# Latent keys and values of a gated-mixer layer, made with positions on partitions instead of channels on partitions, with another order of the first loads and steps and another price for narrow transfers in the planner

## The chip, the core and the metric

The program runs on one core of one Trainium2 chip. A time is the device time of one execution in microseconds. The kernel before took 1004.93 us in the median of 3 runs (999.37 to 1005.2). The profile is that of one further execution, which took 1003.57 us; the span between its first and last instruction is 1001.8 us, so 1.77 us lie around the span.

The engines are named as in the profile: PE (TensorE, with PEld for its weight loads), DVE (VectorE), ACT (ScalarE), POOL (GpSimd) and SP (SyncE, which issues nearly all DMAs).

## The reference, cut to what matters

One layer with 1024 positions plus 16 learned "meta" positions in front (L = 1040), width 1024, all in float32:

```python
h = rms_norm(h_res, pre_norm_g)            # over the 1024 channels of a position
z = h @ w_in                               # one projection, 7328 columns
(pv, pg, cq, ckv, kr, mg, cu, cg, sbcx, sg, gl) = split_cols(z)
...
kv = rms_norm(ckv, kv_norm_g) @ w_ukv      # ckv: 128 columns, over which the norm goes
k_rope = apply_rope(kr, cos, sin)          # kr: 32 columns
k = concat([k_nope, broadcast(k_rope)])    # 8 heads of 64 + 32
...
m = sum_i sigmoid(g_i) * y_i ;  out = h_res + rms_norm(m @ w_o, post_norm_g)
```

Four mixers (pooling, latent attention, a depthwise convolution of 31 taps, a short convolution) read slices of `z`. The change concerns the 160 columns `ckv` (128) and `kr` (32): the latent that keys and values are made from, and the one rotary key that all heads share.

## The kernel before, in words

**Three stages.** Stage one (until about 653 us) normalises x, projects it by `w_in`, and runs the mixers' element-wise work beside the projection. Stage two (about 653 to 870 us) is the attention of 8 heads in two halves of 512 queries each, with the output projections of three branches ("fills") between its matmuls. Stage three is the output projection of the attention, the gated sum, `w_o` and the last norm.

**The projection.** The normalised x is turned so that channels are on partitions, and split into a rounded high part and a rest (`hi`, `lo`), so that a float32 product is three matmuls (hi by hi, hi by lo, lo by hi). x is taken as a matrix of two by two blocks (512 channels by 512 positions: `B11`, `B21`, `B12`, `B22`), and 256 columns of `w_in` make a two by two block of weights; a Winograd scheme does the block product with 7 products instead of 8 from the blocks and their sums `T1` to `T4` (`unit`, `sums_of`, `prep`). `B12` and `T3` share a buffer, which holds `B12` first. A product is 12 matmuls: 4 groups of 128 channels by 3. The weights stand still in PE, up to 512 positions move. The first pairs of columns go in two pieces of 256 and 272 positions (`U0`, `U1`).

**The first 160 columns.** They are done first and directly, since `T1` to `T4` aren't made yet (`plain`): for each of 2 pieces and 2 halves of the positions, 24 matmuls for the 128 latent columns (`ps_pa<-B,kv`) and 24 for the rotary key (`ps_pb<-B,kr`, 64 columns, because its two halves are put beside it in swapped order). The result has channels on partitions and goes to `z_ckv` and `z_kr` in DRAM. Much later `task_kv` reads them back, multiplies `kr` by the cosines and sines, and normalises the latent; since the norm goes over partitions, `rs_row` sums the squares with matmuls by a column of ones and turns the result back with transposes.

**The start.** x comes in 8 tiles of 128 positions (`load_x`, 512 KB each) on SP's queue, with the weights of the 160 columns between. `parts(t)` squares two tiles on ACT, takes the root on POOL (one `pow` for both tiles), scales on DVE, transposes on PE (`ps_x`, `ps_y`), and splits: hi on ACT, lo on DVE. POOL makes the block sums (`x<-x`) in place.

**What orders the work.** No order is written out. `Plan` records every operation with a cost in ns, and at each `flush` gives each engine, in a simulated time, the ready operation of lowest priority number; `plan.ahead(n)` moves operations up by n places in priority. Each engine then runs its list strictly in that order. Two rules of it bear on the change. First, up to the end of the first pair of columns (`keep_busy`), whenever the plan has nothing for PE it puts in a transpose of the identity that nobody reads (`ps_w<-ident`); these are instructions like any other and run even if the real work is ready by then. Second, a DMA has a planned length (L279), bytes times a rate over 16 engines, one after the other, and work that needs it is planned after that. The side work of stage one (`task_kv`, `task_q`, `task_conv` and others) are generators that are pumped a step at a time between products.

In the attention, `load_kv` brings the keys of the next head (`kt<-k`, 64 partitions, 520 KB) once the head before last has been read for the last time, since there are two buffers (`kt0`, `kt1`); `maxima` reads the keys first (`ps_s<-kt,qt`), `attend` next (`ps_s<-qt,kt`). The names in the profile are these program names without numbers; all recorded operations have the line L332.

Of the kernel before, what the change touches and what calls it, by code (L numbers as in the profile page):

```python
# [21 lines left out]
F32 = mybir.dt.float32  # L22
# [171 lines left out]
class Plan:  # L194
# [243 lines left out]
def trunk_kernel(ctx, tc, a):  # L438
# [47 lines left out]
    POOL.memset(f(ends), 0.0)  # L486

    z_dram = {}
    for n in ("a0", "a1", "g0", "g1", "ckv", "kr", "pv0", "pv1", "c0", "c1", "x0", "x1"):
# [67 lines left out]
    def prep(c):  # L557
# [10 lines left out]
        w = {n: blk(src, n) for n, src in (("A11", a11), ("S2", s2), ("S1", s1), ("S3", a21))}  # L568
        sub(DVE, s2, a12, s2)
        w.update({n: blk(src, n) for n, src in (("A12", a12), ("A22", a22), ("S4", s2))})  # L570
        return w

    def product(ps, w, b, c0, n, start, stop):

        for k in range(KH):
            s = slice(c0, c0 + n)
            xh, xl = HB[b][:, 0, k, s], HB[b][:, 1, k, s]
            last = stop and k == KH - 1
            PE.matmul(ps, w[:, 0, k], xh, start=start and k == 0, stop=False, skip_group_check=True)
            PE.matmul(ps, w[:, 0, k], xl, start=False, stop=False, skip_group_check=True)  # L580
            PE.matmul(ps, w[:, 1, k], xh, start=False, stop=last, skip_group_check=True)
# [127 lines left out]
    def load_x(t):  # L709

        xt[t] = (t4([P, D], name="x") if t in (4, 5, 6, 7) else
                 wp.tile([P, D], F32, tag="raw", bufs=3, name="x") if t == 0 else
                 wp.tile([P, D], F32, tag="blk", bufs=7, name="x"))
        SP.dma_start(xt[t], a["x"][0, P * t:P * (t + 1), :])
    g8 = wr.tile([KD, P], F32, tag="wraw", bufs=2, name="g8")

    with plan.slow(-400):
        load_x(0)
        ACT.dma_start(g8, a["pre_norm_g"][0].rearrange("(k p) -> k p", p=P))
        load_x(4)  # L720
        load_x(1)
        load_x(5)
        raw_kv = [wload(i, C_CKV, P + 32) for i in range(2)]
        for t in (2, 6, 3, 7):
            load_x(t)
        xm = wp.tile([NM, D], F32, tag="blk", bufs=7, name="xm")
        SP.dma_start(xm, a["meta_tokens"])
# [34 lines left out]
    def parts(t):  # L762


        for e in range(2):
            square(xt[t + 4 * e], 2 * t + e)
        rsqrt_mean(rsx[:, 2 * t:2 * t + 2], ssx[:, 2 * t:2 * t + 2], D)
        for e, bs in enumerate(((B11, B21), (B12, B22))):
            scaled(xt[t + 4 * e], 2 * t + e)
            for i, b in enumerate(bs):  # L770
                operand_of(b, t, xt[t + 4 * e][:, 512 * i:512 * (i + 1)])
# [9 lines left out]
            operand_of(b, t, src)  # L781

    def meta():
        square(xm, 8)
        rsqrt_mean(rsx[:NM, 8:9], ssx[:NM, 8:9], D)
# [12 lines left out]
        DVE.scalar_tensor_tensor(HB[T1][:, 1, :, 512:], b1, -1.0, f(hi), op0=ALU.mult, op1=ALU.subtract)  # L798
# [18 lines left out]
    parts(0)

    for t in raw_kv:
        POOL.tensor_copy(t[:, :, P + 32:P + 48], t[:, :, P + 16:P + 32])  # L820
        POOL.tensor_copy(t[:, :, P + 48:P + 64], t[:, :, P:P + 16])
    w_kv = [[blk(t[:, :, :P], "kv")] for t in raw_kv]
    kr = wp.tile([P, 2, 2, KH, 64], F32R, tag="blk", bufs=7, name="kr")
# [4 lines left out]
    out_kv = [out_raw(("ckv", "kr"), *u) for u in (U0, U1)]  # L828
    parts(2)
    parts(3)  # L830
# [9 lines left out]
    plain(w_kv, *U1, out_kv[1])  # L840
    for t in range(2, 4):
        operand_of(T3, t, xt[t + 4][:, :512])
    prow = w1([P, P], name="prow")
# [9 lines left out]

    done = {"ckv", "kr"}

    def rs_row(sqs, of, scale=None, tag="x"):

# [235 lines left out]

    def task_kv():

        k0, k1, cs = t4([32, L], name="kr0"), t4([32, L], name="kr1"), t4([32, L], name="kcs")
        for k_, r0, i in ((k0, 0, 0), (k1, 32, 1)):
            ld(k_, z_dram["kr"][r0:r0 + 32, :])  # L1100
            ld(cs, a["trig"][i][:32, :])
            mul(POOL, k_, k_, cs)
            cs = t4([32, L], name="kcs2") if i == 0 else None
        add(POOL, k0, k0, k1)
        yield
        kh, kl = t4([33, L], F32R, name="krh"), t4([33, L], F32R, name="krl")
# [6 lines left out]
            for r, s, n in ((0, 16, 16), (16, 0, 16), (32, 32, 1)):  # L1113
                ld(kr_dram[1][r:r + n, i], t[s:s + n])
        yield
        ckv, sq = t4([P, L], name="ckv"), t4([P, L], name="sqk")
        ld(ckv, z_dram["ckv"])
        ACT.activation(sq, ckv, AF.Square)
        yield
        for n0, n in CH_KV:  # L1120
            rs = yield from rs_row([sq[:, n0:n0 + n]], P)
            DVE.scalar_tensor_tensor(ckv[:, n0:n0 + n], ckv[:, n0:n0 + n], par[:, R_KVG:R_KVG + 1], rs,
                                     op0=ALU.mult, op1=ALU.mult)
        yield
# [68 lines left out]
    def lane(*tasks):  # L1193

        for needs, task, *args in tasks:
# [3 lines left out]
            while True:  # L1199
# [549 lines left out]
```

## Time and profile before

| | |
|---|---|
| median of 3 runs | 1004.93 us (999.37 to 1005.2) |
| profiled execution | 1003.57 us, of it 1001.8 us span |
| PE | 980.2 us busy (98%), 5128 matmuls, 109 of them identity fill |
| PEld | 825.9 us (82%) |
| DVE, ACT, POOL | 657.2 (66%), 463.0 (46%), 701.2 (70%) |
| DMA | 204.54 MB, mean 204 GB/s |
| mean granted PE clock | 0.996 |

How to read it: "busy" counts an engine's own instructions; the profile shows for each what ended the idle time before it. A line of the timeline is "start, length, engine, line, operation, out<-in, form, count", where neighbours of one kind are merged. Matmuls overlap, so the time that one takes from the next is the distance of the starts, not the length shown. "PEclk" is the clock that PE was granted, as a share of the full one.

### The profile page before, as it was taken

Reading aid. Unit: us, or ns where it says so; the run is one execution under the profiler, and the core shown is the slowest. Engines: PE = TensorE matmul, PEld = TensorE weight load, DVE = VectorE, ACT = ScalarE, POOL = GpSimd, SP = SyncE. Lnnn points to the kernel's source line nnn. Section 1 sums busy time; section 2 is a strip of 40 time slices with the busy share of each in tenths; the row PEclk is TensorE's granted clock in tenths of the full one; section 3 lists DMA queues with packets and bytes.
Section 4 is the critical chain, followed back from the end, with each engine's and each line's share of the span. In section 5 each row is a group of like instructions: output and inputs, shape, how many; then the busy total and the mean of one; then the engine's idle time right before and its main releaser. Section 6 shows DMA issues by size and latency. Waiting matters only on the chain. (4 is left out here: it accounts for less than half of the span.)

```text
span 1001.8 us, 15300 instructions
## 1 busy us (share of the span) xinstructions
PE 980.2 (98%) x5128; PEld 825.9 (82%) x5128; DVE 657.2 (66%) x1078; ACT 463.0 (46%) x934; POOL 701.2 (70%) x648
## 2 busy tenths in 40 slices
PE   9999999999999999999999999999989999999996
PEld 9999898889888788777788888878878888788885
DVE  5846686997789769756555223175656656787747
ACT  7543334444444454444445443257656566224631
POOL 6759877766788787698868544236678898536946
PEclk9999999999999999999999999999999999999998
DMA  7269866788778858765665445677678765681624
GB/s 249 85 196 299 269 185 188 234 265 300 238 242 271 259 173 246 229 184 177 197 177 179 132 140 164 227 237 226 181 180 262 209 177 159 227 283 47 219 87 168
DMA packets 128098, 204.54 MB, mean 204 GB/s; under 512 B 19712, under 2 KB 80887, under 8 KB 126674
## 3 DMA queue, kind: packets, MB, share of 16 engines
q1 hardware_dynamic: 123396, 186.79, 60.0%
q10 hardware_dynamic: 4336, 15.73, 4.3%
q8 instruction: 40, 0.66, 0.3%
q0 software_dynamic: 288, 1.05, 0.3%
q14 instruction: 38, 0.31, 0.1%
HBM read 128.98 MB, written 74.56 MB: 203 GB/s over the span
## 5 line engine op out<-in xcount | busy, mean ns | idle before, releaser
L332 PE MATMUL ps_pa<-B,A 128*128 128x512 f32 (+2 forms) x792 | 172.4, 362 | 0.0
L332 PE MATMUL ps_pb<-T,S 128*128 128x512 f32 (+2 forms) x792 | 171.7, 362 | 0.0
L332 POOL TENSOR_TENSOR A<-raw,A 128x512 fp32r<-128x512 f32 x84 | 114.9, 1371 | 72.3 <-ACT A L332 59.4
L332 POOL TENSOR_TENSOR S<-ss,S 128x512 fp32r<-128x512 f32 x84 | 117.0, 1401 | 60.4 <-ACT S L332 58.9
L332 PEld LDWEIGHTS ps_pa<-B,A 128*128 128x128 f32 x792 | 134.4, 188 | 23.5
L332 PEld LDWEIGHTS ps_pb<-T,S 128*128 128x128 f32 x792 | 134.0, 188 | 23.9 <-issue 0.5
L332 POOL TENSOR_TENSOR pt<-p,pt 128x512 fp32r<-128x512 f32 (+1 forms) x96 | 96.6, 1031 | 37.2 <-PE ps_s L332 20.7
L332 ACT ACTIVATE S<-ss 128x512 fp32r<-128x512 f32 x84 | 51.9, 629 | 104.2 <-DVE ss L332 54.1
L332 PE MATMUL ps_y<-bo,whl 128*128 128x512 f32 x288 | 90.6, 411 | 0.3
L332 DVE SCALAR_TENSOR_TENSOR ps_w<-conv,par,ps_w 128x512 f32<-128x512 f32 x116 | 87.2, 752 | 2.3
L332 PE MATMUL ps_pc<-B,S 128*128 128x512 f32 (+2 forms) x396 | 87.5, 364 | 0.5 <-DVE z L332 0.5
L332 PE MATMUL ps_pd<-T,A 128*128 128x512 f32 (+2 forms) x396 | 87.0, 364 | 0.0
L332 PE MATMUL ps_pc<-T,S 128*128 128x512 f32 (+2 forms) x396 | 84.7, 361 | 0.0
L332 PEld LDWEIGHTS ps_pd<-T,A 128*128 128x128 f32 x396 | 67.0, 188 | 12.8 <-issue 1.4
L332 PEld LDWEIGHTS ps_pc<-B,S 128*128 128x128 f32 x396 | 66.9, 188 | 12.8 <-DVE z L332 0.7
L332 PEld LDWEIGHTS ps_pc<-T,S 128*128 128x128 f32 x396 | 67.1, 188 | 11.8
L332 PE MATMUL ps_s<-qt,kt 97*128 97x512 f32 (+4 forms) x336 | 70.1, 326 | 1.0 <-ACT qt L332 0.7
L332 ACT ACTIVATE A<-raw 128x512 fp32r<-128x512 f32 x84 | 52.7, 627 | 37.0 <-PE ps_pd L332 30.1
L332 PE MATMUL ps_o<-pt,vt 128*128 128x512 f32 (+7 forms) x288 | 69.7, 344 | 0.1
L332 ACT ACTIVATE p<-ps_s 128x512 f32<-128x512 f32 (+4 forms) x112 | 49.6, 443 | 35.2 <-DVE ps_s L332 14.6
L332 PEld LDWEIGHTS ps_s<-qt,kt 97*128 97x128 f32 (+1 forms) x336 | 54.1, 176 | 12.0 <-ACT qt L332 1.8
L332 DVE TENSOR_REDUCE mxs<-ps_s 128x1 f32<-128x144 f32 (+6 forms) x112 | 56.1, 507 | 7.7 <-PE ps_s L332 5.4
(354 smaller groups left out, 1905.2 us busy)
## 6 DMA issues: line engine op xcount, KB each, us to landing
raw<-in_w_in_dram SPq DMA_DIRECT2D x56, 512.0 KB
th<-th SPq DMA_DIRECT2D x32, 512.0 KB
th<-z ACTq DMA_DIRECT2D x30, 512.0 KB
v<-vhl SPq DMA_DIRECT2D x16, 384.0 KB
qt<-q SPq DMA_DIRECT2D x16, 384.0 KB
vt<-v SPq DMA_DIRECT2D x8, 768.0 KB
bo<-bo SPq DMA_DIRECT2D x6, 1024.0 KB
kt<-k SPq DMA_DIRECT2D x8, 520.0 KB
```

Of the source, the lines that this page charges most:

```text
L332: getattr(self.handle[o["eng"]], o["op"])(*map(real, o["args"]), **{k: real(v) for k, v in o["kw"].items()})
```

## The change

What it does:

- **Positions on partitions.** `kv_tile(t)` takes the place of `plain`. For each of 9 tiles (8 of 128 positions, one of the 16 meta positions) the x block is the standing operand and the weights move: 160 columns hi and 160 columns lo side by side (320) under x hi, then 160 columns hi under x lo. The two sums stand in two slots of one PSUM bank and are added later. The weights' hi and lo are put into the buffer of `T4`, which is not yet in use. The tile goes to DRAM as `zkv`, positions first.
- **Norm where it stands.** `task_kv` reads `zkv` back with positions on partitions, adds the two slots on POOL, normalises along the free direction (a reduction on DVE, two `pow`, no matmul), and only then turns rope key and latent to channels on partitions, with 18 transposes.
- **The start.** The weights of the 160 columns are loaded after two x tiles instead of four; the first x tile no longer takes a buffer of the weights; `parts` takes root and square tile by tile, and ahead by 2000; a `kv_tile` stands right behind each `parts`; in the first `prep` the block `A12` is split second instead of fifth.
- **The planner's price of narrow transfers.** A DMA whose SBUF side has fewer than 128 rows is planned at up to twice the length (`min(2, P / rows)`), so that 64 rows count as half rate. This touches no DMA itself, only when the planner expects it, in all three stages.

```diff
+ZKV = P + 32
...
-            return {"SP": 450, "ACT": 350, "POOL": 1000}[eng], n * max(0.0432, 0.0235 + 35 / run) / 16
+            rows = (w if getattr(getattr(v, "buf", None), "dram", True) else v).shape[0]
+            return {"SP": 450, "ACT": 350, "POOL": 1000}[eng], n * max(0.0432 * min(2, P / rows), 0.0235 + 35 / run) / 16
...
+    zkv_dram = dram.tile([P, 9, 2 * ZKV], F32, name="zkv")
...
-    def plain(w, c0, n, out):
-
-        for j, bs in enumerate(((B11, B21), (B12, B22))):
-            for i, m in enumerate((P, 64)):
-                ps = bank(("pa", "pb")[i])[:m, :n]
-                for h, b in enumerate(bs):
-                    product(ps, w[h][i], b, c0, n, h == 0, h == 1)
-                with plan.ahead(EVAC):
-                    out(i, j, ps, None, None)
+    def kv_tile(t, n=P):
+
+        bs, c = ((B11, B21), (B12, B22))[t // 4 % 2], slice(512, 512 + n) if t == 8 else slice(P * (t % 4), P * (t % 4 + 1))
+        ps = bank(("pa", "pb")[t % 2])[:n, :2 * ZKV].rearrange("p (s c) -> p s c", s=2)
+        for i, b in enumerate(bs):
+            for k in range(KH):
+                w = HB[T4][:, :, k, ZKV * i:ZKV * (i + 1)]
+                PE.matmul(ps, HB[b][:, 0, k, c], w, start=(i + k == 0), stop=False, skip_group_check=True)
+                PE.matmul(ps[:, 0], HB[b][:, 1, k, c], w[:, 0], start=False, stop=(i + k == KH), skip_group_check=True)
+        with plan.ahead(EVAC):
+            z = up.tile([P, 2, ZKV], F32, tag=("u2", "u3")[t % 2], name="zkv")[:n]
+            copy(z, ps)
+            ld(zkv_dram[:n, t], z)
...
         load_x(4)
-        load_x(1)
-        load_x(5)
-        raw_kv = [wload(i, C_CKV, P + 32) for i in range(2)]
-        for t in (2, 6, 3, 7):
+        raw_kv = [wload(i, C_CKV, ZKV) for i in range(2)]
+        for t in (1, 5, 2, 6, 3, 7):
             load_x(t)
...
-        for e in range(2):
-            square(xt[t + 4 * e], 2 * t + e)
-        rsqrt_mean(rsx[:, 2 * t:2 * t + 2], ssx[:, 2 * t:2 * t + 2], D)
+        with plan.ahead(2000):
+            for i in (2 * t, 2 * t + 1):
+                square(xt[t + 4 * (i % 2)], i)
+                rsqrt_mean(rsx[:, i:i + 1], ssx[:, i:i + 1], D)
...
     for i, t in enumerate(raw_kv):
-        split(kr[:, i, 0], kr[:, i, 1], t[:, :, P:P + 64])
-        w_kv[i].append(kr[:, i])
-    parts(1)
...
+        hi, lo = (HB[T4][:, s, :, ZKV * i:ZKV * (i + 1)] for s in range(2))
+        copy(hi, t[:, :, :ZKV])
+        sub(POOL, lo[:, :, 32:], t[:, :, :P], f(hi[:, :, :P]))
+        sub(POOL, lo[:, :, :32], t[:, :, P:ZKV], f(hi[:, :, P:]))
+    for t in range(4):
+        parts(t)
+        kv_tile(t)
+        kv_tile(t + 4)
     meta()
-    plain(w_kv, *U0, out_kv[0])
+    kv_tile(8, NM)
...
-    w = prep(C_CU)
+    w = prep(C_CU, True)
...
     def task_kv():
...
+        zk, zm = w1([P, 8, 64], name="zk"), w1([NM, 2 * ZKV], name="zm")
+        ld(zk, zkv_dram[:, :8, P:P + 64])
+        ld(zm, zkv_dram[:NM, 8])
+        z0 = t4([P, 8, P], name="z0")
+        ld(z0, zkv_dram[:, :8, :P])
+        sq = t4([P, 8, P], name="sqk")
+        ld(sq, zkv_dram[:, :8, P + 64:])
...
-        ckv, sq = t4([P, L], name="ckv"), t4([P, L], name="sqk")
-        ld(ckv, z_dram["ckv"])
-        ACT.activation(sq, ckv, AF.Square)
-        yield
-        for n0, n in CH_KV:
-            rs = yield from rs_row([sq[:, n0:n0 + n]], P)
...
+        rs = rsx[:, :9]
+        ACT.activation(sq, z0, AF.Square)
...
+        DVE.tensor_reduce(rs[:, :8], sq, axis=AX.X, op=ALU.add)
+        rsqrt_mean(rs[:, :8], rs[:, :8], P)
...
+        mul(POOL, z0, z0, rs[:, :8].unsqueeze(2).to_broadcast([P, 8, P]))
...
+            pt, c = turn(i, [z0[:, 4 * i + j] for j in range(4)] if i < 2 else [zm[:, :P]], P)
+            DVE.tensor_scalar(ckv[:, c], pt, par[:, R_KVG:R_KVG + 1], None, op0=ALU.mult)
```

How it moves instructions, at two places. The first is PE at the start, from the first transposes of x to the products of the 160 columns. `ps_w` is the identity fill, `ps_x` and `ps_y` are transposes of x, `kv` and `kr` the weights of the 160 columns; in the changed kernel `T_238` is the buffer of `T4`, which holds these weights. Before:

```order
L332 MATMUL ps_w<-ident 128x128 x6
L332 MATMUL ps_x<-ident,x 128x128 x4
L332 MATMUL ps_w<-ident 128x128 x43
L332 MATMUL ps_y<-ident,x 128x128 x4
...
L332 MATMUL ps_pa<-B_268,kv 128x256
L332 MATMUL ps_pb<-B_268,kr 64x256
L332 MATMUL ps_w<-ident 128x128 x4
```

Changed:

```order
L334 MATMUL ps_w<-ident 128x128 x19
L334 MATMUL ps_x<-ident,x 128x128 x4
L334 MATMUL ps_w<-ident 128x128 x2
L334 MATMUL ps_y<-ident,x 128x128 x4
L334 MATMUL ps_w<-ident 128x128 x3
L334 MATMUL ps_x<-ident,x 128x128 x4
L334 MATMUL ps_w<-ident 128x128 x3
L334 MATMUL ps_pa<-T_238,B_258 128x320
L334 MATMUL ps_w<-ident 128x128 x2
L334 MATMUL ps_x<-ident,x 128x128 x4
L334 MATMUL ps_pa<-T_238,B_258 128x160
```

The products of the 160 columns begin after 12 transposes of x instead of 28, the block of 43 fill transposes is gone, and the fill counts 85 over the whole program instead of 109.

The second place is SP in the attention, at the load of head 4's keys (`kt0<-k2`; `whl`, `th` and `rb` are loads for the fills and the softmax sums, `qt` are queries, `vt` values). Before:

```order
L332 DMA r1_7707<-lc_7586 128x8
L332 DMA whl_7739<-w_out_conf20_1968 128x512
L332 DMA rb_7745<-r1_7707 64x1024
L332 DMA th_7752<-th16_5721 128x1024
L332 DMA qt_7761<-q0_4473 96x1024
L332 DMA kt0_6797<-k2_2613 64x2080
L332 DMA vt0_6799<-v1_3679 128x1536
```

Changed:

```order
L334 DMA th_7561<-th6_4659 128x1024
L334 DMA r1_7641<-lc_7530 128x8
L334 DMA qt_7674<-q0_4431 96x1024
L334 DMA kt0_6746<-k2_2661 64x2080
L334 DMA whl_7689<-w_out_conf10_1941 128x512
L334 DMA rb_7699<-r1_7641 64x1024
L334 DMA th_7703<-th7_4626 128x1024
```

The three loads `whl`, `rb` and `th` that stood between the store `r1` and the queries now stand behind the keys.

More of the change, by code (lines that the diff above doesn't have):

```diff
@@ L488, in trunk_kernel @@
     z_dram = {}
-    for n in ("a0", "a1", "g0", "g1", "ckv", "kr", "pv0", "pv1", "c0", "c1", "x0", "x1"):
+    zkv_dram = dram.tile([P, 9, 2 * ZKV], F32, name="zkv")
+    for n in ("a0", "a1", "g0", "g1", "pv0", "pv1", "c0", "c1", "x0", "x1"):
         z_dram[n] = dram.tile([P, L], F32, name=f"z_{n}")
@@ L555, in blk, with prep @@
         return b
-    def prep(c):
+    def prep(c, early=False):
         (a11, a21), (a12, a22) = ((t[:, :, :P], t[:, :, P:]) for t in (wload(0, c), wload(1, c)))
@@ L567, in prep @@
         sub(DVE, a21, a11, a21)
-        w = {n: blk(src, n) for n, src in (("A11", a11), ("S2", s2), ("S1", s1), ("S3", a21))}
+        w = {n: blk(src, n) for n, src in (("A11", a11),) + (("A12", a12),) * early + (("S2", s2), ("S1", s1), ("S3", a21))}
         sub(DVE, s2, a12, s2)
-        w.update({n: blk(src, n) for n, src in (("A12", a12), ("A22", a22), ("S4", s2))})
+        w.update({n: blk(src, n) for n, src in (("A12", a12),) * (not early) + (("A22", a22), ("S4", s2))})
         return w
@@ L711, in load_x @@
         xt[t] = (t4([P, D], name="x") if t in (4, 5, 6, 7) else
-                 wp.tile([P, D], F32, tag="raw", bufs=3, name="x") if t == 0 else
                  wp.tile([P, D], F32, tag="blk", bufs=7, name="x"))
@@ L783, in meta @@
     def meta():
-        square(xm, 8)
-        rsqrt_mean(rsx[:NM, 8:9], ssx[:NM, 8:9], D)
+        with plan.ahead(2000):
+            square(xm, 8)
+            rsqrt_mean(rsx[:NM, 8:9], ssx[:NM, 8:9], D)
         scaled(xm, 8)
@@ L816, in nopump @@
         pass
[L817 to L823, printed above, removed]
-    for i, t in enumerate(raw_kv):
-        split(kr[:, i, 0], kr[:, i, 1], t[:, :, P:P + 64])
-        w_kv[i].append(kr[:, i])
-    parts(1)
-    out_kv = [out_raw(("ckv", "kr"), *u) for u in (U0, U1)]
-    parts(2)
-    parts(3)
+    for i, t in enumerate(raw_kv):
+        hi, lo = (HB[T4][:, s, :, ZKV * i:ZKV * (i + 1)] for s in range(2))
[6 more added lines that the diff above has]
+        kv_tile(t + 4)
     meta()
-    plain(w_kv, *U0, out_kv[0])
+    kv_tile(8, NM)
     for t in range(2):
         sums_of(t)
-    w = prep(C_CU)
+    w = prep(C_CU, True)
     for t in range(2):
@@ L839, in trunk_kernel @@
         sums_of(t)
-    plain(w_kv, *U1, out_kv[1])
     for t in range(2, 4):
@@ L851, in trunk_kernel @@
         DVE.tensor_scalar(par[:, r0:r0 + n], par[:, r1:r1 + n], 0.5, None, op0=ALU.mult)
-    done = {"ckv", "kr"}
+    done = set()
     def rs_row(sqs, of, scale=None, tag="x"):
@@ L1096, in task_kv, with turn @@
     def task_kv():
[L1098 to L1103, printed above, removed]
+        zk, zm = w1([P, 8, 64], name="zk"), w1([NM, 2 * ZKV], name="zm")
[5 more added lines that the diff above has]
+        ld(sq, zkv_dram[:, :8, P + 64:])
+        k1, k0 = (t4([32, L], name=n) for n in ("kr1", "kr0"))
+        ld(k0, a["trig"][0][:32, :])
+        ld(k1, a["trig"][1][:32, :])
+        yield
+        krs = [(zk, zk[:, :, :32], zk[:, :, 32:]),
+               (zm[:, P:P + 64], zm[:, P:ZKV], zm[:, ZKV:ZKV + 32])]
+        for _, x, y in krs:
+            add(POOL, x, x, y)
+        add(POOL, zm[:, :P], zm[:, :P], zm[:, P + 64:])
+        add(POOL, z0, z0, sq)
+        for i, (_, x, y) in enumerate(krs):
+            for r, s in ((0, 16), (16, 0)):
+                u, v = (y[:, :, r:r + 16], x[:, :, s:s + 16]) if i == 0 else (y[:, r:r + 16], x[:, s:s + 16])
+                POOL.tensor_copy(u, v)
+        yield
+        def turn(part, srcs, n):
+            pt = bank()[:n]
+            for j, src in enumerate(srcs):
+                m = src.shape[0]
+                PE.transpose(pt[:, m * j:m * (j + 1)], src, ident[:m, :m])
+            m = sum(src.shape[0] for src in srcs)
+            return pt[:, :m], slice(NM + 512 * part, NM + 512 * part + m) if part < 2 else slice(0, m)
+        for i in range(3):
+            pt, c = turn(i, [zk[:, 4 * i + j] for j in range(4)] if i < 2 else [zm[:, P:P + 64]], 64)
+            mul(DVE, k0[:, c], pt[:32], k0[:, c])
+            mul(DVE, k1[:, c], pt[32:], k1[:, c])
+            yield
         add(POOL, k0, k0, k1)
@@ L1115, in task_kv @@
         yield
-        ckv, sq = t4([P, L], name="ckv"), t4([P, L], name="sqk")
-        ld(ckv, z_dram["ckv"])
-        ACT.activation(sq, ckv, AF.Square)
+        rs = rsx[:, :9]
+        ACT.activation(sq, z0, AF.Square)
+        ACT.activation(zm[:, P + 64:], zm[:, :P], AF.Square, accum_out=rs[:NM, 8:])
+        DVE.tensor_reduce(rs[:, :8], sq, axis=AX.X, op=ALU.add)
+        rsqrt_mean(rs[:, :8], rs[:, :8], P)
+        rsqrt_mean(rs[:NM, 8:], rs[:NM, 8:], P)
         yield
-        for n0, n in CH_KV:
-            rs = yield from rs_row([sq[:, n0:n0 + n]], P)
-            DVE.scalar_tensor_tensor(ckv[:, n0:n0 + n], ckv[:, n0:n0 + n], par[:, R_KVG:R_KVG + 1], rs,
-                                     op0=ALU.mult, op1=ALU.mult)
+        mul(POOL, z0, z0, rs[:, :8].unsqueeze(2).to_broadcast([P, 8, P]))
+        DVE.tensor_scalar(zm[:, :P], zm[:, :P], rs[:NM, 8:], None, op0=ALU.mult)
         yield
+        ckv = t4([P, L], name="ckv")
+        for i in range(3):
+            pt, c = turn(i, [z0[:, 4 * i + j] for j in range(4)] if i < 2 else [zm[:, :P]], P)
+            DVE.tensor_scalar(ckv[:, c], pt, par[:, R_KVG:R_KVG + 1], None, op0=ALU.mult)
+            yield
         ch, cl = t4([P, L], F32R, name="ckh"), t4([P, L], F32R, name="ckl")
@@ L1208, in trunk_kernel @@
         lane(*[((f"a{m}", f"g{m}"), task_conv, m, c) for c in range(2) for m in range(2)]): 0.9,
-        lane(*[((), task_so, k) for k in range(KH)], (("ckv", "kr"), task_kv), (("cq0", "cq1"), task_q, 0), ((), task_q, 1),
+        lane(*[((), task_so, k) for k in range(KH)], ((), task_kv), (("cq0", "cq1"), task_q, 0), ((), task_q, 1),
              ): 0.8,
```

## The prediction

> **What bounds the kernel now.** I read the page first, then who made PE wait, then the clock in small windows round the longest wait, then PE's list at the start.
>
> ```profile
> PE 980.2 (98%) x5128; PEld 825.9 (82%) x5128; DVE 657.2 (66%) x1078; ACT 463.0 (46%) x934; POOL 701.2 (70%) x648
> ```
>
> PE is busy nearly always. So only three things are worth time: real PE work taken away, fill transposes taken away (they count as busy), and waits of PE. The waits, over the whole program:
>
> ```profile
> PE ps_s L332 <- DMA kt<-k: 3.3, 1, 3.3
> PE ps_y L332 <- DVE lcp L332: 1.5, 2, 1.1
> PE ps_x L332 <- issue: 0.8, 1, 0.8
> PE ps_pc L332 <- DVE z L332: 0.5, 1, 0.5
> ```
>
> One is large: PE waits 3.3 us for the keys of head 4. Here is the matmul that waited, and then the windows round it (columns: length, then busy time of PE, PEld, DVE, ACT, POOL; then the granted clock):
>
> ```profile
> 736.16 0.66 PE L332 MATMUL ps_s<-kt,qt 96*128 96x144 f32 x3 [3.28 <-DMA kt<-k]
> ```
>
> ```profile
> 734.00:736.00 2.00, 0.00 (x0) 0.00 (x0) 0.05 (x1) 0.00 (x0) 1.84 (x3) 1.00 0.90 214
> 736.00:738.00 2.00, 1.84 (x9) 1.67 (x10) 1.43 (x5) 0.00 (x0) 0.73 (x1) 0.79 1.02 278
> 738.00:740.00 2.00, 2.00 (x9) 1.46 (x8) 1.30 (x3) 0.45 (x1) 0.00 (x0) 0.50 0.30 77
> 740.00:742.00 2.00, 2.00 (x10) 1.69 (x9) 1.08 (x3) 0.77 (x2) 1.06 (x1) 0.86 0.87 232
> ```
>
> After the wait the clock is below one for three windows: 2 x (0.21 + 0.50 + 0.14) = 1.7 us of PE time are lost on top. The wait costs 3.3 + 1.7 = 5.0 us.
>
> At the start the timeline of PE shows how much is no real work:
>
> ```profile
> 13.27 4.86 PE L332 MATMUL ps_w<-ident 128*128 128x128 f32 x43
> 18.33 0.63 PE L332 MATMUL ps_y<-ident,x 128*128 128x128 f32 x4 [0.20 <-issue]
> ...
> 28.51 1.57 PE L332 MATMUL ps_pa<-T,kv 128*128 128x256 f32 x12
> 29.92 0.75 PE L332 MATMUL ps_pa<-B,kv 128*128 128x256 f32 x5
> ...
> 54.04 1.66 PE L332 MATMUL ps_pb<-T,kr 128*64 128x272 f32 x12
> 55.54 1.67 PE L332 MATMUL ps_pb<-B,kr 128*64 128x272 f32 x12
> 57.05 0.60 PE L332 MATMUL ps_x<-ident,x 128*128 128x128 f32 x4
> 57.48 0.60 PE L332 MATMUL ps_y<-ident,x 128*128 128x128 f32 x4
> 57.84 1.65 PE L332 MATMUL ps_pa<-B,A 128*128 128x256 f32 x12
> ...
> 77.76 1.58 PE L332 MATMUL ps_pa<-B,A 128*128 128x256 f32 x12
> ```
>
> From these starts: a fill transpose takes (18.33 - 0.20 - 13.27) / 43 = 0.113 us, a matmul with 256 moving 1.41 / 12 = 0.1175, with 272 moving 1.50 / 12 = 0.125 whether 128 or 64 columns stand, a transpose 0.43 / 4 = 0.108. The first Winograd product starts at 57.84 us and the second pair of columns at 77.76. None of the larger waits above lies in the rest of stage one, so what is saved before 77.76 is kept as long as the rest holds.
>
> **The change, part by part.** The sum is made against the profiled execution, 1003.57 us, which is 1.36 us below the median of the runs.
>
> *Products of the 160 columns.* Removed: 2 pieces x 2 halves x 48, that is 96 x 0.1175 + 96 x 0.125 = 23.3 us. Added: 9 tiles x 8 pairs of one matmul with 320 and one with 160 moving. For 320 I go from 256 towards 512:
>
> ```profile
> 102.56 2.94 PE L332 MATMUL ps_pb<-T,S 128*128 128x512 f32 x12
> 105.34 2.01 PE L332 MATMUL ps_pc<-T,S 128*128 128x512 f32 x8
> ```
>
> 512 take 2.78 / 12 = 0.232, so a column is 0.114 / 256 us and 320 take 0.146. The trace has no 160; the nearest rows have 144 columns:
>
> ```profile
> 684.74 0.46 PE L332 MATMUL ps_s<-qt,kt 97*128 97x144 f32 x3
> 685.03 0.44 PE L332 MATMUL ps_y<-bo,whl 128*128 128x512 f32 x1
> ...
> 688.01 0.34 PE L332 MATMUL ps_o<-pt,vt 128*128 128x144 f32 x2
> 688.18 0.34 PE L332 MATMUL ps_s<-kt,qt 96*128 96x272 f32 x1
> ```
>
> These are 0.29 / 3 = 0.097 and 0.17 / 2 = 0.085 us, more than 144/256 of a 256. Ends: 0.085 below, 0.1175 (a 256) above; I take 0.100, near the first row, which has the same kind of standing operand. 72 x (0.146 + 0.100) = 17.7 us, **5.6 us saved** (4.3 to 6.7). [...]
>
> *Fill.* 109 become 85 in the order: 24 x 0.113 = **2.7 us saved**. It is fixed by the order, so it is certain as PE work; whether waits take its place is the term after the next.
>
> *Norm of the latent.* The row of its sums of squares, grouped by form:
>
> ```profile
> L332 PE MATMUL ps_x<-ones,sqk 128*128 128x1 f32 x16 | 1.9, 240 | 0.0
> ```
>
> They go (1.9 us), with 8 transposes of 0.108 (0.9); 16 transposes come (1.7); the small ones of the meta positions, on both sides, are left out. **1.1 us saved**. The new work on POOL, DVE and ACT (adds, a reduction, two `pow`) costs nothing while `task_q`, which follows it, is done long before the attention: in the trace the last query product is at 529.86 and the attention begins at 653.8, over 120 us of cover.
>
> ```profile
> 529.86 1.54 PE L332 MATMUL ps_x<-cqn,whl 128*128 128x512 f32 x6
> ...
> L332 PE MATMUL ps_s<-kt,qt x112: 230/338/476, 653.8 to 837.3; 96*128 96x264 f32 x16, 96*128 96x328 f32 x16, 96*128 96x392 f32 x16, 96*128 96x456 f32 x16
> ```
>
> *Does the start get its data in time?* PE's list up to the first Winograd product now sums to 1.4 (start) + 81 x 0.113 + 76 x 0.108 + about 1.6 (gain and meta transposes) + 17.7 = 38 us, with 52 transposes now behind it. POOL is the closest. Its prices:
>
> ```profile
> 7.64 0.71 POOL L332 TENSOR_TENSOR rsx<-rsx,mhalf 128x2 f32<-128x2 f32 x1 [5.81 <-DVE rsx L332]
> ...
> 19.30 10.65 POOL L332 TENSOR_TENSOR x<-x 128x512 f32<-128x512 f32 x8
> ...
> 58.80 1.29 POOL L332 TENSOR_TENSOR S<-ss,S 128x512 fp32r<-128x512 f32 x1
> ```
>
> Nine `pow` at 0.71 instead of five (6.4), lo of the weights (twice 640 elements at 1.29 per 512, 3.2), 16 sums at 1.33 (21.3), seven splits at 1.29 (9.0), two `whl` of 256 elements (1.3): 41.2 us. They began at 7.64 and begin no later now, with one square ahead of the first root instead of two; so they end near 48.8 if POOL never waits. PE asks for the last of them (`S4`) after 38 + 9.0 (72 matmuls with 256 and 4 with 272 moving) + 52 x 0.108 + 0.5 of fill = 53 us. That leaves 4 us for POOL's waits in its list; before, the split ended at 58.80 + 1.29 = 60.1 and now it must be 7 us earlier. The start's waits of PE in the list above are 0.8 (`issue`) and 0.5 (`z`); with a fifth less fill to cover them I add **1.0 us lost** (0 to 3).
>
> *Loads and the price of narrow transfers.* The 160 columns' weights come two x tiles earlier, x1 and x5 later; ACT squares x1 only after two splits of weights, so that is hidden behind ACT. Nine stores of 160 KB replace six, all on SP, which idles then. The planner's price moves the attention's loads. SP's rows before head 4's keys:
>
> ```profile
> 723.60 0.32 SPq L332 DMA_DIRECT2D whl<-w_out_conf  x1
> 724.09 0.45 SPq L332 DMA_DIRECT2D rb<-r  x1
> 724.59 0.58 SPq L332 DMA_DIRECT2D th<-th  x1
> 725.27 0.37 SPq L332 DMA_DIRECT2D qt<-q  x1
> 725.69 0.45 SPq L332 DMA_DIRECT2D kt<-k  x1
> ```
>
> PE needs the keys at 736.16 less 3.3, 7.2 us after their issue, behind four loads issued in the 2 us before. For head 2 the keys follow the queries alone, and there was no wait:
>
> ```profile
> 678.50 0.32 SPq L332 DMA_DIRECT2D qt<-q  x1
> 678.86 0.45 SPq L332 DMA_DIRECT2D kt<-k  x1
> ...
> 687.94 0.23 PE L332 MATMUL ps_s<-kt,qt 96*128 96x144 f32 x1
> ```
>
> There 9.1 us were enough. In the new order `whl`, `rb` and `th` stand behind head 4's keys, which therefore neither queue behind them nor wait for `whl`'s release on PE. I take the wait as gone: **5.0 us saved** (0 to 5.0, and below nothing if another head's keys come late). What is late next is a vector step of the kind of `lcp` (1.5 us), as before.
>
> Sum: 1003.57 - 5.6 - 2.7 - 1.1 + 1.0 - 5.0 = **990.2, say 990 us**.
>
> **The rivals.** *The keys stay late* at head 4, or one other head takes its place. For it: the price only shifts the plan, the loads still share the same engines, and the new order has `whl` ahead of head 5's and head 6's keys. Against it: head 2 had this same order and no wait. Then 990 + 5 = 995 us.
>
> *The start becomes bound by POOL.* If its own waits come to more than those 4 us, PE runs out of operands; at the far end the saving before the second pair (5.6 + 2.7 - 1.0 = 7.3) turns into waits: 997 us. For it: the slack is 4 us in 49. Against it: what PE needs first (`A11`, `A12`, the sums of the first half) is early in POOL's list. [...]
>
> *Slower.* The new plan places the first key product of each head by planned landings. If three or more of the six heads 2 to 7 get their keys as late as head 4 did, at 5.0 us each, the sum is 990 + 15 = 1005 and more; from the third on it decides. Against it: the PE work between the last reading of a key buffer and the first reading of its new content is about the same in both orders, and only one head missed before. With waits a little longer than here, 1016.
>
> **How the numbers follow.** 1% is about what a measurement of this kernel can tell from no change; it is 10 us here, so faster means below 994.9 and slower above 1015. The forecast has 0.65, its own range 986 to 995 (matmul saving at 6.7 and the start's waits at 0 give 988, and 986.6 if `lcp` goes too; matmul saving at 4.3 and 3 us of waits at the start give 993.5, another small wait 995). Of it 0.62 lie below 994.9. Late keys: 0.17, of which 0.05 below. POOL: 0.12, of which 0.01 below. Slower than before: 0.06, of which 0.05 beyond 1%. Faster 0.68, same 0.03 + 0.12 + 0.11 + 0.01 = 0.27, slower 0.05. The range goes from 984 to 1000, which takes in the forecast and both rivals on this side.
>
> **What would show it.** In the changed profile: 85 identity transposes; 72 matmuls of 320 and 72 of 160, whose starts are 0.25 us apart per pair; the first `ps_pa<-B,A` near 39 to 41 us and the second pair near 70 instead of 77.76; no `ones,sqk`; no wait on `kt<-k` and a clock of 1.00 round 725; PE at 98% or more of a span near 988. I am wrong if the second pair starts later than 74 (the start is fed too slowly), if a pair of new matmuls takes 0.29 or more, or if a wait on `kt<-k` stands in the list.

## The result, and the profile after

The changed kernel takes 988.02 us (median of 4 runs, 986.46 to 988.91) against 1004.94 us (4 runs, 999.37 to 1005.2): a ratio of 0.9843, 95% interval [0.9807, 0.9879]. Forecast were 990, in 984 to 1000. The profiled execution took 986.46 us with a span of 984.7, 17.1 less than the span before. The first line of the page, and the head of the list of who made PE wait:

```profile
PE 968.4 (98%) x5047; PEld 814.0 (83%) x5047; DVE 666.8 (68%) x1089; ACT 463.5 (47%) x935; POOL 701.2 (71%) x654
```

```profile
PE ps_y L334 <- DVE lcp L334: 1.5, 2, 1.0
...
PE ps_s L334 <- DMA kt<-k: 0.4, 1, 0.4
```

PE is as full as before and has 81 instructions fewer. The wait of 3.3 us for the keys of head 4 is gone; one of 0.4, at head 1, is there instead. Where the 17.1 us lie is read from three landmarks: the first product of the second pair of columns, the first score of the attention, and the first product behind the attention. From PE's timeline and the groups by tile, after:

```profile
66.95 1.46 PE L334 MATMUL ps_pa<-B,A 128*128 128x256 f32 x11
```

```profile
L334 PE MATMUL ps_s<-kt,qt x112: 228/337/476, 641.9 to 823.1; 96*128 96x264 f32 x16, 96*128 96x328 f32 x16, 96*128 96x392 f32 x16, 96*128 96x456 f32 x16
```

```profile
L334 PE MATMUL ps_u<-boM,whl x192: 388/392/477, 852.4 to 896.2; 128*128 128x512 f32 x192
```

and the last of them before:

```profile
L332 PE MATMUL ps_u<-boM,whl x192: 387/392/476, 869.6 to 913.4; 128*128 128x512 f32 x192
```

The second pair starts at 66.95 instead of 77.76: 10.8 us come from the start. The attention starts at 641.9 instead of 653.8, 11.9 earlier, so the rest of stage one gave 1.1. The product behind it starts at 852.4 instead of 869.6, 17.2 earlier, so the attention gave 5.3. Nothing comes behind that.

How the 10.8 us are made up stands in one window each, before and after, from 2 us to the start of the second pair's `ps_pb<-T,S` (80.69 and 69.89; columns as in the prediction, behind the clock the busy share of the DMA engines and GB/s):

```profile
2.00:80.69 78.69, 76.59 (x627) 74.65 (x625) 49.47 (x86) 44.22 (x92) 50.91 (x47) 1.00 0.57 185
```

```profile
2.00:69.89 67.89, 67.56 (x555) 66.25 (x554) 52.17 (x88) 42.72 (x89) 50.06 (x46) 1.00 0.61 198
```

PE's busy time falls by 9.0 us, with 72 instructions fewer (48 products and 24 fill transposes), and its idle time from 2.1 to 0.33 us.

### The profile page after: what moved, and what is told of

Its sections match the earlier page's. It is cut to its first block, busy times and chain, and to the rows that moved or that the text cites. A ratio compares the mean times of both kernels' runs of the same rounds, so it can differ in the third digit from the quotient of the medians.

```text
span 984.7 us, 15157 instructions
## 1 busy us (share of the span) xinstructions
PE 968.4 (98%) x5047; PEld 814.0 (83%) x5047; DVE 666.8 (68%) x1089; ACT 463.5 (47%) x935; POOL 701.2 (71%) x654
## 4 chain that ended last, share of the span: by engine, by line
PE 89%; DVE 5%; DMA 2%; issue 1%; POOL 1%; ACT 1%; SPq 0%; DVEq 0%; ACTq 0%; POOLq 0%
PE ps_pb L334 15%; PE ps_pa L334 15%; PE ps_pc L334 15%; PE ps_o L334 10%; PE ps_y L334 8%; PE ps_s L334 7%; PE ps_pd L334 7%; PE ps_u L334 7%; PE ps_x L334 3%; DVE ps_w L334 1%; PE ps_w L334 1%; DMA kt<-k 1%; DMA z_cg<-z 1%; DVE z L334 1%; POOL x L334 1%
## 5 line engine op out<-in xcount | busy, mean ns | idle before, releaser
L334 PE MATMUL ps_pb<-T,S 128*128 128x512 f32 (+2 forms) x792 | 175.6, 364 | 0.0
L334 PE MATMUL ps_pc<-T,S 128*128 128x512 f32 (+2 forms) x396 | 87.0, 363 | 0.0
```

Of the source, the lines that this page charges most:

```text
L334: getattr(self.handle[o["eng"]], o["op"])(*map(real, o["args"]), **{k: real(v) for k, v in o["kw"].items()})
```

## The experiments

Theory: the start gave what PE no longer has to do, and the attention what the new price of narrow loads moved on SP's queue. Rivals: the keys came in time only because everything before them moved; the start was won by the order of loads or of the roots; fill is not work on the path (on the chain that sets the time) at all.

**The price alone, in both directions.** In the changed kernel the old price, and in the kernel before the new one:

```
-  n * max(0.0432 * min(2, P / rows), 0.0235 + 35 / run) / 16
+  n * max(0.0432, 0.0235 + 35 / run) / 16
```

> The changed kernel with the old price of a load (a 64-row load priced at full rate), all else as changed. My theory: the price alone took away the wait for head 4's keys, because the old plan puts whl, rb and th ahead of them on SP's queue. Then the wait on kt<-k comes back (about 3.3 us, with a lower clock behind it), and the time is 5 us above the changed kernel: 992 to 994, while the first Winograud-step product (ps_pa<-B,A) still starts near 41. Rival, the wait went because everything before it moved: no kt<-k wait above 1 us, time 987 to 989. Rival, the price costs something elsewhere: below 987.

> The kernel before with only the new price of 64-row loads. My theory: its kt<-k wait of 3.3 us and the clock loss behind it go, 5 us saved of 1004.9: 999 to 1000.5, start unchanged (first ps_pa<-B,A near 57.8). Rival, the price does nothing by itself: 1004 to 1006 with the wait in the list.

The first measured 995.07 us (8 runs, 989.93 to 1001.25; ratio to before 0.9907 [0.9874, 0.994]), the second 998.79 (12 runs, 997.33 to 1000.93; 0.9942 [0.9926, 0.9959]). Beside 0.9843 for the whole change the price is worth 0.6% of 1005 in either place, some 6 us. Both medians lie just outside the ranges expected, and the runs with the old price in the changed kernel spread over 11 us, so that its interval still touches that of the whole change; the interval of the second is clear of 1. In the second the keys are not in the list of waits. With the old price in the changed kernel the wait was back, while the first Winograd product still started at 40.70: its row in the list, the matmul at head 4, and the windows behind it:

```profile
PE ps_s L334 <- DMA kt<-k: 6.0, 3, 3.9
```

```profile
725.79 0.89 PE L334 MATMUL ps_s<-kt,qt 96*128 96x144 f32 x3 [3.91 <-DMA kt<-k]
```

```profile
724.00:726.00 2.00, 0.21 (x2) 0.24 (x3) 0.00 (x0) 0.00 (x0) 1.65 (x2) 1.00 0.90 257
726.00:728.00 2.00, 2.00 (x9) 1.80 (x9) 1.76 (x6) 0.00 (x0) 0.00 (x0) 0.51 0.96 229
728.00:730.00 2.00, 2.00 (x10) 1.46 (x9) 0.87 (x2) 0.26 (x1) 0.00 (x0) 0.64 0.18 47
```

The clock loss behind it is 2 x (0.49 + 0.36) = 1.7 us, as in the kernel before. Here the keys of head 5 (1.4 us) and head 1 (0.7) were late too. SP's rows show what the price does. With the old price:

```profile
712.61 0.32 SPq L334 DMA_DIRECT2D whl<-w_out_conf  x1
713.10 0.45 SPq L334 DMA_DIRECT2D rb<-r  x1
713.60 0.58 SPq L334 DMA_DIRECT2D th<-th  x1
714.27 0.37 SPq L334 DMA_DIRECT2D qt<-q  x1
714.69 0.45 SPq L334 DMA_DIRECT2D kt<-k  x1
```

and in the changed kernel, whose attention begins within 0.2 us of the same time:

```profile
710.03 0.32 SPq L334 DMA_DIRECT2D qt<-q  x1
710.40 0.45 SPq L334 DMA_DIRECT2D kt<-k  x1
711.74 0.32 SPq L334 DMA_DIRECT2D whl<-w_out_conf  x1
712.22 0.45 SPq L334 DMA_DIRECT2D rb<-r  x1
712.77 0.53 SPq L334 DMA_DIRECT2D th<-th  x1
```

The keys go 4.3 us earlier, ahead of the three loads. Of these, 1.7 us are the issues of the three loads, and 2.6 that the group begins later, with `whl` at 712.61 instead of the queries at 710.03; what SP waited for there is not shown. With the old price they were usable 725.79 - 714.69 = 11.1 us after their issue; PE had asked for them 3.9 us before.

**Whose price it is.** The price for the keys' loads alone:

```
-  0.0432 * min(2, P / rows)
+  0.0432 * (min(2, P / rows) if v.shape[-1] == 2080 else 1)
```

and, in another kernel, a still higher price:

```
-  0.0432 * min(2, P / rows)
+  0.0432 * (3 if rows <= 64 else 1)
```

> The changed kernel with the new price for the keys' loads alone (64 rows of 2080), all other 64-row loads at the old price. With the old price everywhere 995.1 was measured, with the new one 988.0. Theory: it is the planned landing of the keys themselves that puts their load ahead of whl, rb and th on SP's queue at head 4; then there is no kt<-k wait above 1 us and the time is 987 to 990. Rival: the prices of the other narrow loads (rb, the weights of the keys, parts of q) are needed too: a wait on kt<-k stays and the time is 992 to 996.

> The changed kernel with a still higher price, three times full rate for loads of 64 rows or fewer. If twice is near the truth, there is nothing left to win and other loads are pushed back without need: 987 to 990. Rival: keys still land later than planned at twice, the small waits that are left (kt<-k 0.4, qt 0.3) go, and it is faster: below 986.5. Second rival: th and whl come late now: above 990 with waits on them.

The keys' price alone gave 988.12 (5 runs, 985.27 to 990.5; ratio 0.9845 [0.9816, 0.9873]), within the noise the same as the whole price. Head 4's keys were issued right behind the queries (716.05) and it did not wait, so the planned landing of the keys is what moves them. The expectation was wrong in one thing: a wait of 1.7 us on the keys stood at head 1 instead. Three times gave 986.21 (984.35 to 989.99; 0.983 [0.9804, 0.9857]). Its median is below the 986.5 that the first rival asked for, but inside the interval of the changed kernel measured beside it (0.9847 [0.9821, 0.9873]), and its waits on the keys were 1.1 us, more than 0.4 and not gone: neither rival is shown.

**The order of the first loads and of the roots.** First the old order of loads, then the old roots (two at a time, not ahead of other work; the root of the meta positions isn't ahead either, not shown here), then both:

```
-  raw_kv = [wload(i, C_CKV, ZKV) for i in range(2)]
-  for t in (1, 5, 2, 6, 3, 7):
+  load_x(1)
+  load_x(5)
+  raw_kv = [wload(i, C_CKV, ZKV) for i in range(2)]
+  for t in (2, 6, 3, 7):
       load_x(t)
```

```
-  with plan.ahead(2000):
-      for i in (2 * t, 2 * t + 1):
-          square(xt[t + 4 * (i % 2)], i)
-          rsqrt_mean(rsx[:, i:i + 1], ssx[:, i:i + 1], D)
+  for e in range(2):
+      square(xt[t + 4 * e], 2 * t + e)
+  rsqrt_mean(rsx[:, 2 * t:2 * t + 2], ssx[:, 2 * t:2 * t + 2], D)
```

> The changed kernel with the old order of loads at the start: x1 and x5 ahead of the weights of the 160 columns. My theory (the start is bound by PE's own list of products, transposes and fill; the plan has 83 fill transposes here against 85): within 2 us of the changed kernel, 986 to 990. Rival, the earlier weights are what lets PE work densely from 12 us on: 3 us or more lost, 991 or above, seen as waits of PE or POOL before 41 us.

> The changed kernel with the roots of x's norms taken two at a time and not ahead of other work, as before. The plan then has 104 fill transposes instead of 85. My theory (fill in the list is PE time, 0.113 us each, where PE does not wait): 19 x 0.113 = 2.1 us lost, 989.5 to 991. Rival, fill only stands where PE would wait anyway, so that roots taken early give nothing: 987 to 989. Rival, POOL's fewer pow (five instead of nine, 2.8 us) let the sums come earlier: below 987.

> The changed kernel with both the old order of loads and the old roots, so that of the start only the new form of the products is left (with the new price). The two alone measured 986.6 and 989.0 against 988.0. My theory: nearly all that the start gained comes from the products, so the time stays at 987 to 990.5 and the attention begins at 641 to 646 instead of 653.8. Rival, each of the two edits covers for the other, and without both the start loses what it gained: 993 or above, attention from 648 on.

Old loads: 986.56 (6 runs, 984.31 to 989.46; 0.9822 [0.9792, 0.9852]). Old roots: 989.01 (6 runs, 988.5 to 989.46; 0.9842 [0.9813, 0.9872]), just under the range of my theory and at the upper end of the first rival's. The attention began at 644.5, 2.6 later than in the changed kernel's profile, but the times don't show it, and two profiles of the unchanged kernel differ by 1.2 us there (641.9 and 643.1). Both: 990.76 (5 runs, 989.09 to 992.88; 0.9866 [0.9844, 0.9889]), the attention at 645.1:

```profile
L334 PE MATMUL ps_s<-kt,qt x112: 228/332/472, 645.1 to 825.8; 96*128 96x264 f32 x16, 96*128 96x328 f32 x16, 96*128 96x392 f32 x16, 96*128 96x456 f32 x16
```

So without the two orders 8.7 of the 11.9 us up to the attention are there, and the two together are worth 2 to 3 us, with intervals that overlap. The 8.7 aren't the new form of the products and of the norm alone: the `kv_tile` behind each `parts`, the earlier `A12` and the price are still in, and no run takes out the first two. The median lies just over the 990.5 I had given. The old loads were measured again beside the changed kernel on one chip:

> The changed kernel once more, unchanged, on the same chip as the next one: 987 to 989 as before. In two profiles the same small idle of PE at the head starts (about 0.65 us within 4 us) went with a clock of 0.8 for 8 us and in one it did not; if that is what spreads the times of one kernel, its runs fall into groups about 1.7 us apart.

> The changed kernel with the old order of loads once more, beside the changed kernel on the same chip. There it measured 986.6 against 988.0 elsewhere, and its attention began 1.9 us earlier (640.0 against 641.9). If that is real, it is 1 to 2 us below the run beside it; if it was another chip or a chance of the clock, the two are within 0.5 us.

989.35 (5 runs, 987.16 to 989.63; 0.9847 [0.9821, 0.9873]) and 988.76 (5 runs, 984.59 to 988.96; 0.9843 [0.9817, 0.9868]). The medians are 0.6 apart and the lowest times 2.6; the changed kernel's median is just above the 987 to 989 expected. The record has the mean granted clock of every run, and it sorts these times. With the old loads the 4 runs at 0.997 took 984.31 to 985.13 us and the 7 at 0.991 to 0.993 took 987.93 to 989.46; the changed kernel's 4 runs at 0.997 took 986.46 to 988.91. So where the clock held, the old order was over 1 us quicker, and in 7 of 11 runs it lost that again to the clock. Why it loses clock more often is open, and it is not shown that it makes a better kernel.

**Is PE's own work what the start costs?** More of it, less of it, and no fill. The first widens the second matmul of a pair to 320 columns (the product of the two low parts is added), the second removes that line (the product of x's low parts with the weights' high parts is left out), the third leaves out the fill transposes:

```
-  PE.matmul(ps[:, 0], HB[b][:, 1, k, c], w[:, 0], start=False, stop=(i + k == KH), skip_group_check=True)
+  PE.matmul(ps, HB[b][:, 1, k, c], w, start=False, stop=(i + k == KH), skip_group_check=True)
```

```
-  PE.matmul(ps, HB[b][:, 0, k, c], w, start=(i + k == 0), stop=False, skip_group_check=True)
-  PE.matmul(ps[:, 0], HB[b][:, 1, k, c], w[:, 0], start=False, stop=(i + k == KH), skip_group_check=True)
+  PE.matmul(ps, HB[b][:, 0, k, c], w, start=(i + k == 0), stop=(i + k == KH), skip_group_check=True)
```

```
-  plan.keep_busy("transpose", warm, ident, ident)
+  pass
```

> The changed kernel with the second matmul of each pair 320 columns wide instead of 160 (it adds the product of the two low parts). A pair then takes 2 x 0.146 = 0.292 us by my price of 320 columns, against a measured pair of about 0.26. My theory, the start is bound by PE's work: 72 x 0.032 = 2.3 us lost, 989.5 to 991.5. Rival, the 160 is not cheaper than what its weight load allows, and nothing is lost: 987.5 to 988.5. Rival, the start waits for its data and wider matmuls take the place of fill: also 987.5 to 988.5, but with a pair of 0.29 in the rows.

> The changed kernel without the 160-column matmuls; it leaves out the product of x's low parts with the weights' high parts. 72 matmuls at 0.114 go, 8.2 us; the plan puts 117 fill transposes in place of 85, 32 x 0.113 = 3.6 us. If the start is bound by PE's list: 988.0 - 8.2 + 3.6 = 983.4, so 982 to 985. Rival, bound by the feed of x (loads, norms, scaling, sums on POOL): waits take the place, 986.5 to 988.5.

> The changed kernel without any fill transposes (one initial one stays), 84 x 0.113 = 9.5 us of PE time. My term for fill took each one as PE time on the path; by that the time falls by up to 9.5 us, to 979 to 984. Rival, fill stands only where PE would wait, and keeps the clock up: PE waits instead, the second pair of columns starts at 69 to 71 as now, and the time is 987 to 990. Second rival, the waits lower the granted clock too: 991 or above, with a clock below 0.9 in windows of the first 40 us.

Wide: 991.67 (5 runs, 990.97 to 992.49; 0.9876 [0.9855, 0.9896]), some 3.3 us by the ratios. Four pairs of the changed kernel, from 30.57 to 31.61, and the same piece of the wide one, from 32.49 to 33.68:

```profile
30.57 1.20 PE L334 MATMUL ps_pa<-T,B 128*128 128x320 f32 x8
31.61 0.60 PE L334 MATMUL ps_y<-ident,x 128*128 128x128 f32 x4
...
37.96 1.93 PE L334 MATMUL ps_pa<-T,B 128*16 128x320 f32 x16
39.72 0.49 PE L334 MATMUL ps_y<-ident,x 128*128 128x128 f32 x3
...
41.05 1.21 PE L334 MATMUL ps_pa<-B,A 128*128 128x256 f32 x8
```

```profile
32.49 1.35 PE L334 MATMUL ps_pa<-T,B 128*128 128x320 f32 x8
33.68 0.93 PE L334 MATMUL ps_x<-ident,x 128*128 128x128 f32 x7
...
43.71 1.67 PE L334 MATMUL ps_pa<-B,A 128*128 128x256 f32 x12
```

A pair takes 1.04 / 4 = 0.26 us, a wide one 1.19 / 4 = 0.30; the first Winograd product comes 2.7 us later (2.66 / 72 = 0.037 a pair). What PE is given to do there, it pays in full. Taking away pays less: without the second matmul 984.89 (4 runs, 984.61 to 986.3; 0.9811 [0.9787, 0.9834]), 3.2 us by the ratios. 8.2 us of matmuls went and 3.6 of fill came (117 in place of 85), so 4.6 were to be had; the time is still inside the 982 to 985 that I gave for a start bound by PE's list. The first Winograd product stands at 37.57, 3.5 earlier (the second pair, at 65.36, only 1.6 earlier):

```profile
37.57 1.65 PE L334 MATMUL ps_pa<-B,A 128*128 128x256 f32 x12
```

And without fill 987.89 (5 runs, 984.65 to 988.12; 0.9824 [0.9798, 0.985]): the same, as the first rival said. PE's rows without it:

```profile
7.22 1.12 PE L334 MATMUL ps_x<-ident,x 128*128 128x128 f32 x4 [1.75 <-DVE rsx L334]
8.13 1.06 PE L334 MATMUL ps_y<-ident,x 128*128 128x128 f32 x4
8.98 1.06 PE L334 MATMUL ps_x<-ident,x 128*128 128x128 f32 x4
...
15.89 2.21 PE L334 MATMUL ps_pa<-T,T 128*128 128x320 f32 x8 [0.53 <-ACT zkv L334]
17.90 1.05 PE L334 MATMUL ps_y<-ident,x 128*128 128x128 f32 x4
...
20.64 0.60 PE L334 MATMUL ps_x<-ident,x 128*128 128x128 f32 x4
20.99 0.40 PE L334 MATMUL ps_pb<-T,B 128*128 128x320 f32 x1
...
41.16 1.07 PE L334 MATMUL ps_pa<-B,A 128*128 128x256 f32 x7
```

The first Winograd product starts at 41.16 against 41.05, although PE ran at half pace until past 17.90: four transposes took 8.13 to 8.98, 0.85 us, and later 20.64 to 20.99, 0.35. The equal times hide two parts. The first product into `ps_pb`, at 20.99 without fill, stood at 19.00 with it:

```profile
19.00 0.35 PE L334 MATMUL ps_pb<-T,B 128*128 128x320 f32 x1
```

So up to there the kernel without fill falls 2.0 us behind (with four more transposes of x done, 0.4 us). From there to the first Winograd product it takes 20.2 us against 22.1. The changed kernel has 14 fill transposes in that stretch, 14 x 0.113 = 1.6 us; with the four transposes that makes 2.0, against the 1.9 measured. Behind 19 us fill cost its full price. Ahead of it 67 fill transposes went with the full pace from 6.50 us on (four transposes in 0.46 us); without them, at half pace, PE came to the same work 1.6 us later. The stretch from 6 to 20 us, without fill and with it:

```profile
6.00:20.00 14.00, 11.91 (x51) 11.23 (x52) 9.16 (x18) 9.92 (x19) 11.90 (x15) 1.00 1.05 354
```

```profile
6.00:20.00 14.00, 14.00 (x121) 14.00 (x120) 9.55 (x20) 11.56 (x22) 11.30 (x14) 1.00 1.05 354
```

PE has 121 instructions or 51 there, and the DMA engines are full (354 GB/s) in both. But no engine waits for x's loads in most of it: the last wait for one ends at 6.13 us with fill and at 5.72 without. With fill ACT and POOL are busy for 11.56 and 11.30 of the 14 us; without it PE, at half pace, and POOL for 11.91 and 11.90. Which of them sets the pace up to 19 us is not settled. Behind 20 us PE works without a wait in the kernel without fill, so there its own list is the limit.

## Why the prediction was right, step by step

The forecast's sum, 990.2, stands against 986.46 in the profiled execution. Of the 3.7 us between them 2.8 are one term with the wrong sign (the start's waits), 0.7 the start's work and 0.3 the keys. By the medians the change won 16.9 us where the sum had 13.4. The mechanisms that carried it, the products and the keys' place in the queue, were right; the reason given for one term, fill, was not, and one term, the norm, has the right number by luck. Of the three signs of being wrong one came up: a wait on `kt<-k` of 0.4 us stands in the list (0.9 in the second profile), at head 1, which did not wait before. The pairs at 0.26 us and the second pair at 66.95 are on the right side.

*Products, -5.6.* 64 pairs of 0.26 and, with 16 columns standing, 8 of 1.76 / 8 = 0.22 make 18.4 us, not 17.7. The 160-column matmul costs, with 320 at 0.146, 0.26 - 0.146 = 0.114 us, near my upper end (a 256) and not near the 144 row that I chose. By these pairs the saving is 23.3 - 18.4 = 4.9. What was removed cost more than I priced, however: PE's busy time fell by 9.0, and by 6.3 without the 24 fill transposes. I took 0.1175 from an unbroken dozen; where transposes stood between, as here in the kernel before, eight took 1.04 us, 0.13 each:

```profile
21.27 1.20 PE L332 MATMUL ps_pa<-B,kv 128*128 128x256 f32 x8
22.31 0.60 PE L332 MATMUL ps_x<-ident,x 128*128 128x128 f32 x4
```

PE's list up to the first Winograd product, which the prediction summed to 38 us, took 41.05: among other things the first 17 fill transposes took 5.18 - 1.36 = 3.8 us, 0.225 each and not 0.113. The forecast was made from the differences and did not use that sum.

*Fill, -2.7, "certain as PE work".* This step had the wrong reason: what a fill transpose costs depends on where it stands. In the kernel before, all 109 stood ahead of 21 us. In the changed kernel 67 stand ahead of 19 us, and 18 behind, of which the kernel without fill shows 14 at their full price. The block of 43 that went had covered a stretch, 13.27 to 18.33, in which ACT and POOL (fourth and fifth busy time) were full with splits, squares, roots and a sum of x; no engine waited for x's loads behind 8.79 us. Before:

```profile
12.00:16.00 4.00, 4.00 (x40) 4.00 (x37) 2.57 (x5) 3.97 (x10) 4.00 (x6) 1.00 1.05 362
16.00:20.00 4.00, 3.80 (x34) 3.41 (x33) 2.69 (x5) 3.94 (x8) 4.00 (x6) 1.00 0.77 175
```

What the new form does there is to put real work in fill's place: the first product of the 160 columns stood at 20.07 and now stands at 11.57:

```profile
20.07 0.37 PE L332 MATMUL ps_pa<-B,kv 128*128 128x256 f32 x1
```

```profile
11.57 0.40 PE L334 MATMUL ps_pa<-T,B 128*128 128x320 f32 x1
```

That this is why the sum still held is argued, not tested. PE's busy time up to the second pair fell by 9.0 us where products and fill together were put at 8.3.

*The start's waits, +1.0.* This term had the wrong sign: PE's idle time there fell by 1.8 us. POOL, which I had feared, was busy for 50.06 of 67.89 us and made PE wait nowhere in that stretch; the one wait left, 0.3, is on DVE. In the kernel without fill, where no fill covers a wait, POOL made PE wait 0.3 us once, at 10.38. The rival of a start bound by POOL is out. With 2.8 us the start's waits were the largest error. DVE's scaling of x kept its time in the changed kernel: `x<-x,rsx,ps_pc` took 0.75 us at 7.22, where POOL idled, and 0.75 at 14.91, beside one of POOL's sums. DVE's difference `ss<-ss,raw` did not: it took 1.78 us at 37.92 beside POOL's sums, and 0.68 at 58.82, where POOL idled.

*Norm, -1.1.* The rest of stage one gave 11.9 - 10.8 = 1.1, the number forecast, but mostly not by this term. Between the landmarks (80.69 to 653.8, and 69.89 to 641.9) PE's busy time fell by 0.3 us, from 571.81 to 571.54, and its idle time by 0.8, from 1.30 to 0.47. This wait of the kernel before is no longer there:

```profile
463.52 1.13 PE L332 MATMUL ps_y<-pd,pw 128*128 128x512 f32 x2 [1.30 <-DVE pd L332]
```

It is gone too in the kernel before with the new price, and back with 1.2 us with the old price and 1.3 with the keys' price alone, so the price has to do with it; but it stands with 0.9 in the kernel with both old orders, which has the new price. No run tests the norm by itself, and that the number came out is luck.

*Keys, -5.0.* 5.3 by the landmarks of the profiled executions, some 6 us by the runs, which hold what else the price moves. In the profile with the old price three heads' keys were late. That head 4's keys came late by their place behind `whl`, `rb` and `th` is shown by the price put in and taken out, and by the keys' price alone; how much of it is the later issue and how much the sharing of the DMA engines with the three loads is not. The rival of another head's keys as late as head 4's were is out for this order; the 0.4 to 0.9 us at head 1, and 1.7 with the keys' price alone, show that it was not far off.

## What to carry to other kernels

A planner's price of one kind of transfer can be worth as much as a new form of the work: look for the load that PE waited for, what stood ahead of it on its queue, and whether the plan believed it would land in time. Before counting a filler instruction as time saved, ask where it stands: here the 67 ahead of 19 us cost nothing, since without them PE, at half pace, came to the same work 1.6 us later, and that real work moved into their place pays is argued above, not tested; the 14 behind, where PE's own list was the limit, cost their full price, 1.6 us. And DMA engines that are full were not a limit by themselves here: from 6 to 20 us they moved 354 GB/s, and no engine waited for x's loads behind 6.13; look for the engine that waits. Price a broken-up run of matmuls from a broken-up run (0.13 us each here, against 0.1175 in an unbroken dozen), and a narrow one from the nearest wider row as well as from the narrower (160 columns took 0.114 us, with 0.1175 for 256 and 0.097 for 144).

## What the runs showed of the hardware that was not expected

*Behind the same short idle the clock fell to 0.50, or stayed at 1.00.* At the start of head 3 PE idles some 0.76 us, in three pieces within 4 us, in each of these profiles. In the changed kernel's first profile the clock stayed at 1.00; in the one with the old loads, measured again, it did not:

```profile
696.00:700.00 4.00, 3.53 (x26) 2.89 (x25) 3.30 (x12) 1.11 (x5) 1.63 (x4) 1.00 0.77 217
700.00:704.00 4.00, 3.72 (x18) 2.82 (x16) 3.37 (x9) 2.65 (x5) 0.74 (x1) 1.00 0.39 97
```

```profile
696.00:700.00 4.00, 3.24 (x22) 2.45 (x20) 3.46 (x11) 1.34 (x5) 0.78 (x3) 1.00 0.62 159
700.00:704.00 4.00, 4.00 (x10) 3.13 (x11) 2.54 (x7) 2.25 (x4) 0.95 (x1) 0.50 0.59 163
704.00:708.00 4.00, 4.00 (x14) 3.15 (x13) 0.28 (x1) 3.19 (x6) 3.56 (x4) 0.65 0.08 34
```

The loss there is 4 x (0.50 + 0.35) = 3.4 us. The changed kernel's second profile lost half of that at the same place:

```profile
700.00:704.00 4.00, 3.24 (x15) 2.27 (x15) 3.83 (x13) 0.58 (x1) 0.00 (x0) 0.83 0.41 126
704.00:708.00 4.00, 4.00 (x14) 3.20 (x14) 1.03 (x3) 3.84 (x7) 2.57 (x3) 0.74 0.42 131
```

4 x (0.17 + 0.26) = 1.7 us, the same as behind the long waits for keys. At half speed that is 1.7 / 0.5 = 3.4 or 3.4 / 0.5 = 6.8 us, an estimate from these losses; in the profile with the old loads every window of 1 us from 700 to 706 reads 0.50. What decides between the three outcomes behind these 0.76 us is not shown. It fits that one kernel's times fall into groups (987.16 and 987.18, at a mean clock of 0.997, then 989.35 to 989.63, at 0.996); where in the run the clock was lost is known only for the profiled ones.

*The clock column does not show the start.* Without fill PE ran at half pace until past 17.90 us while its windows say 1.00. The same holds for the first 17 fill transposes of the changed kernel, 0.225 us each, against 0.113 later. There the pace has to be read from the distance of the starts.
